# Another order of the expert passes in the first layer, two last passes summed on chip, and the latents' sum and norm ahead of the context's

## The chip, the cores and the metric

The kernel runs on one core of a Trainium2 chip. The metric is device time in microseconds (us) of one execution. Engines are named as in the profile: PE (TensorE; PEld is its weight load), DVE (VectorE), ACT (ScalarE), POOL (GpSimd) and SP (SyncE, which only issues DMAs here).

## The reference, cut to what matters

Two layers over 256 latent and 256 context tokens of width D = 1024 in float32. Each layer has a modulation (`w_mod`), an input projection in three groups of heads, attention, an output projection, and then a mixture of 32 experts (SwiGLU, hidden width 256) of which each token takes two. The output is the latent tokens alone, so the second layer's experts work on 256 tokens and the first layer's on 512. In short:

```python
for l in range(DEPTH):
    x, ctx = attention_block(x, ctx, c, c_ctx, l)    # w_mod, w_in, attention, w_out, DeepNorm
    for t in (x, ctx):
        gates, experts = route(t)                    # top group, then top-2 of its 8 experts
        y = sum(gates[k] * down(silu(up_a(t)) * up_b(t)) for k in experts)
        t = layernorm(ALPHA * t + g2 * y) * lg + lb  # g2 from w_mod, lg and lb from ln_rows
    ...
return x
```

## The kernel before, in words

**Memory.** All large tiles live in 23 units of 128 x 2048 floats (1 MB each), handed out by `Mem`. Weights are loaded in one fixed order (`stream`): `pump()` issues the next load as long as a unit is free and the weights held stay under a cap (`cap[0]`), and it is called after each `drop` of a weight that has been used. Weights of experts whose number is known at build time, and all weights of projections, are issued by SP (L161). The others of layer 0, 28 experts with three units each, are issued by POOL as indirect DMAs (L142), since the order of the experts by load is only known on the chip. An expert's units are called `c0` and `c1` (the two halves of up) and `c2` (down).

**Passes.** A pass is 128 rows of PE. `PLAN` gives their order: P is two experts with 64 rows each, Q four experts with 32 rows, F one expert with 128 rows, and f a second pass of 128 rows of the F before it, with the same weights, which are kept until f is done. Ahead of the list stand two P of fixed experts (the 2 in `PLAN`), so layer 0 has 14 passes, here P P Q F Q f P Q F Q P P P P. They are taken in sets of two, which share one one-hot matrix (`onehot`) and one gather of their rows by PE (`gather`, L1179).

**One pass.** `up` (L1192, with silu and product on ACT and DVE, L1198 and L1199), `mid` (two transposes, L1226), then in layer 0, for all passes but the last, `put`: down (L1237), and the 128 rows of results go to a DRAM buffer `ys` (L1242, by SP). The last pass stays on chip: `back` (L1210 to L1218), `down` (L1250, results split in a high and a low part, L1258 and L1259) and `combine` (L1273, L1278), which brings rows back to tokens by matmuls with the transposed one-hot.

**End of layer 0.** In the last pass, behind its `up`, `fold` reads the two rows of each token back from `ys` (8 indirect DMAs on POOL, L1465, two for each block of 128 tokens), and sums and scales them on ACT and DVE (L1469 to L1472) into the residual `X`. After `combine` comes `rest`, a loop for experts with more rows than their passes hold (L1478, L1479). Its number of turns is read on the chip and is 0 here, but entering it is a barrier for all engines, and what is behind it in the program stands behind it on every engine. Then layer 1 begins: `second` gives the DeepNorm of a block (L425 sum, L416 and L419 moments, L429 and L431, L436 the next norm), first for the two latent blocks. `presplit` splits the first projection weights (`qa`, L449 and L450), L320 multiplies `w_mod`, `turned` transposes the latents (L481 to L499), and L455 to L457 are the matmuls of the first projection. They are three float32r matmuls for one of float32.

**Order on an engine.** Each engine runs its instructions in the order in which a scheduler put them at build time; a scheduler's priority can be raised for a stretch of code (`high_priority`). A DMA is issued by its engine in that order too, and waits there for the memory it writes.

## Time and profile before

| | us |
|---|---|
| three runs | 1121.86, 1124.82, 1124.9 (median 1124.82) |
| profiled execution, own time | 1121.56 |
| its span, first to last instruction | 1119.8 |
| PE busy | 1000.2 (89%) |
| DVE, ACT, POOL busy | 510.2 (46%), 347.3 (31%), 303.3 (27%) |
| moved by DMA | 301.06 MB, mean 269 GB/s |

Busy times are shares of the whole span, over stages that have different limits. The experts of layer 0 run from about 330 to 638 us, layer 1 behind them, its experts to 1106 us. Line numbers (L142) are those of the kernel before, unless a sentence says that they are of the changed kernel.

### The profile page before, as it was taken

What the parts mean: (1) busy time and instruction counts of PE and PEld (TensorE: products, weight loads), DVE (VectorE), ACT (ScalarE), POOL (GpSimd) and SP (SyncE); (2) the same over time, 40 slices, a digit from 0 to 9 for tenths busy, and PEclk for the clock granted to TensorE, in tenths of its full rate; (3) what the DMA queues carried; (4) which work ended last, traced back from release to release, by engine and by line L of the source; (5) the groups of instructions that cost most, each with busy time, mean ns of one, the idle gap of its engine ahead of it and who ended that gap; (6) DMA issues with size and microseconds to landing.
All of it is one profiled execution on the core that took longest, in us unless ns stands there. A gap on an engine that the chain in (4) does not pass through costs nothing. (4 is left out here: it accounts for less than half of the span.)

```text
span 1119.8 us, 14771 instructions
## 1 busy us (share of the span) xinstructions
PE 1000.2 (89%) x5497; PEld 567.9 (51%) x5497; DVE 510.2 (46%) x1369; ACT 347.3 (31%) x707; POOL 303.3 (27%) x326
## 2 busy tenths in 40 slices
PE   4999999999999998999867279999998899999893
PEld 2788744557765553453212158854456554433231
DVE  5644367775575210100001887356665654342244
ACT  4533155553442110111000376134454221211011
POOL 2112134340002412434421222133210045443420
PEclk9999999999999999999999579999998799999997
DMA  9722157420469987899998563356425799999992
GB/s 381 304 73 91 43 207 285 176 76 1 170 272 364 421 357 299 354 422 423 421 421 351 215 221 119 112 201 241 165 76 225 286 363 419 421 421 421 421 421 95
DMA packets 46351, 301.06 MB, mean 269 GB/s; under 512 B 5410, under 2 KB 5794, under 8 KB 14532
## 3 DMA queue, kind: packets, MB, share of 16 engines
q0 software_dynamic: 25824, 177.81, 38.9%
q1 hardware_dynamic: 20452, 122.27, 28.8%
q8 instruction: 45, 0.74, 0.3%
q14 instruction: 30, 0.25, 0.1%
HBM read 292.19 MB, written 7.87 MB: 268 GB/s over the span
## 5 line engine op out<-in xcount | busy, mean ns | idle before, releaser
L142 POOL DMA_INDIRECT u<-in_w_exp,u x162 | 162.0, 1000 | 327.1 <-PE psa L1192 144.0
L1192 PE MATMUL psa<-u,u 128*32 128x512 f32 (+2 forms) x1040 | 221.3, 603 | 16.3 <-DMA u<-in_w_exp,u 16.2
L455 PE MATMUL psa<-u,u 128*128 128x512 f32 (+3 forms) x400 | 141.3, 356 | 1.0 <-ACT u L498 0.7
L456 PE MATMUL psa<-u,u 128*128 128x512 f32 (+3 forms) x400 | 140.4, 352 | 2.0 <-DVE u L450 2.0
L1192 PEld LDWEIGHTS psa<-u,u 128*32 128x32 f32 (+2 forms) x1040 | 65.5, 127 | 146.9 <-issue 109.9
L457 PE MATMUL psa<-u,u 128*128 128x512 f32 (+3 forms) x400 | 139.5, 352 | 0.4 <-DVE u L499 0.3
L1199 DVE TENSOR_TENSOR scr<-scr,psa 128x256 f32<-128x256 f32 x26 | 10.9, 420 | 213.1 <-ACT scr L1198 213.1
L1179 PEld LDWEIGHTS psc<-u,u 128*128 128x128 f32 x640 | 82.7, 197 | 31.5 <-issue 26.5
L878 POOL TENSOR_SCALAR u<-u,ri 128x512 f32<-128x512 f32 (+1 forms) x48 | 68.5, 1431 | 100.2 <-DVE ri L876 82.6
L1179 PE MATMUL psc<-u,u 128*128 128x256 f32 x640 | 92.7, 296 | 3.0 <-DVE u L1165 2.1
L455 PEld LDWEIGHTS psa<-u,u 128*128 128x128 f32 x400 | 75.7, 190 | 12.5 <-ACT u L498 1.1
L456 PEld LDWEIGHTS psa<-u,u 128*128 128x128 f32 x400 | 76.1, 190 | 11.7 <-DVE u L450 3.1
L457 PEld LDWEIGHTS psa<-u,u 128*128 128x128 f32 x400 | 75.6, 190 | 10.0 <-DVE u L499 0.9
L875 ACT ACTIVATE u<-psa,nm 128x512 f32<-128x512 f32 (+1 forms) x96 | 58.4, 615 | 55.8 <-DVE nm L873 50.9
L1198 ACT ACTIVATE scr<-psa 128x256 f32<-128x256 f32 x26 | 10.0, 385 | 192.1 <-PE psa L1192 192.1
L450 DVE TENSOR_TENSOR u<-u,u 128x1024 fp32r<-128x1024 f32 (+4 forms) x38 | 56.2, 1485 | 19.7 <-ACT u L449 19.6
L1237 PE MATMUL pse<-u,scr 128*32 128x512 f32 (+2 forms) x248 | 63.0, 600 | 1.9 <-ACT scr L1227 1.9
L1181 ACT ACTIVATE u<-psc 128x512 f32<-128x512 f32 x52 | 31.1, 597 | 107.9 <-PE psc L1179 69.4
L1250 PE MATMUL pse<-u,scr 128*64 128x512 f32 (+1 forms) x272 | 63.6, 599 | 0.6 <-DMA u<-in_w_exp,u 0.6
L873 DVE TENSOR_REDUCE nm<-psa 128x1 f32<-128x512 f32 (+1 forms) x80 | 53.1, 682 | 14.1 <-PE psa L863 10.5
L419 POOL TENSOR_TENSOR lns<-lns,mhalf 128x1 f32<-128x1 f32 x22 | 14.2, 646 | 149.0 <-DVE lns L418 108.3
L1273 PE MATMUL psa<-u,u 128*128 128x512 f32 x112 | 38.4, 458 | 17.1 <-DVE u L1278 11.0
(315 smaller groups left out, 1360.3 us busy)
## 6 DMA issues: line engine op xcount, KB each, us to landing
u<-in_w_mod SPq DMA_DIRECT2D x48, 1024.0 KB, 5.9
u<-in_w_exp SPq DMA_DIRECT2D x30, 1024.0 KB, 8.0
u<-in_w_out SPq DMA_DIRECT2D x8, 1024.0 KB, 5.0
ys<-u SPq DMA_DIRECT2D x13, 512.0 KB, 8.3
u<-in_w_in_b SPq DMA_DIRECT2D x10, 512.0 KB, 12.4
u<-in_w_in_v SPq DMA_DIRECT2D x4, 960.0 KB, 4.5
u<-in_w_in_qa SPq DMA_DIRECT2D x4, 768.0 KB, 10.4
u<-in_ln_rows SPq DMA_DIRECT2D x6, 512.0 KB, 5.8
```

Source lines behind the costliest of these rows:

```text
L142: G.indirect_dma_start(out=b.ap(UNIT), out_offset=None, in_=wexp_rows, in_offset=bass.IndirectOffsetOnAxis(ap=idx, axis=0), bounds_check=N ...
L450: V.tensor_tensor(l_[:, c], w[:, c], h[:, c].bitcast(F32), OP.subtract)
L455: PE.matmul(p, lhsT=a[0], rhs=b[0], start=first, stop=False)
L456: PE.matmul(p, lhsT=a[0], rhs=b[1], start=False, stop=False)
L457: PE.matmul(p, lhsT=a[1], rhs=b[0], start=False, stop=final)
L873: V.tensor_reduce(out=nm[:, s, 0:n], in_=pv, axis=AX.X, op=OP.max, negate=True)
L875: S.activation(P[:, i, :], pv[:, i, :], AF.Exp, bias=nm[:, s, i:i + 1], accum_out=su[:, s, i:i + 1])
L878: (G if s == 0 else V).tensor_scalar(P[:, i, :], P[:, i, :], ri[:, s, i:i + 1], None, op0=OP.mult)
L1179: PE.matmul(pv[:, j, :], lhsT=H[b][:, k * 128:(k + 1) * 128], rhs=OH[:, b, :], start=(b == 0 and i == 0), stop=(b == nb - 1 and i == 1))
L1192: PE.matmul(g[r, :], lhsT=XG[:, k, at * 128 + r.start:at * 128 + r.stop], rhs=W(t, k // 4).v(4, 512)[:, k % 4, :], start=(k == 0), stop=(k ...
L1237: PE.matmul(y[r, :], lhsT=hc[:, c * 128 + r.start:c * 128 + r.stop], rhs=W(t, 2).v(2, D)[:, c, f * 512:f * 512 + 512], start=(c == 0), sto ...
L1250: PE.matmul(y[r, :], lhsT=hc[:, c * 128 + r.start:c * 128 + r.stop], rhs=W(t, 2).v(2, D)[:, c, f * 512:f * 512 + 512], start=(c == 0), sto ...
```

## The change

The order of the passes in layer 0 becomes P P Q Q F f Q Q F P P P P P. Two passes stay on chip in place of one (`HOME`); each has its own split result (`parts`), and one PSUM sum takes both, four matmuls in place of two for a block and half. Twelve passes write to `ys`. The reads from `ys` (`fetch`) are issued at the start of the pass before the last and the fold stands behind that pass's up. The caps on the weights are 8 from the fourth last pass on (9 before), 7 from the one before the last (9), 4 in the last and 5 behind it (both as before). The loop `rest` stands ahead of the combine, with a result tile of its own. The combine is done for the two latent blocks first, then their DeepNorm with raised priority, then the combine for the two context blocks (`rest_of`). In passes with `put`, one piece of the next gather is ahead of `mid`.

```diff
-PLAN = ((2, "QFQfPQFQPPPP"), (3, "QPQPQPQPP"))
+PLAN = ((2, "QQFfQQFPPPPP"), (3, "QPQPQPQPP"))
...
-RP = (1, 1)
-LC = (4, 12)
+HOME = 2
+HC = (8, 7, 4, 5)
...
+        def make_h():
+            hT.extend([mem.get(UNIT, F32R) for _ in range(2)] for _ in range(2))
+            HT.extend([h.v(4, 512) for h in x] for x in hT)
+
+        if not last:
+            make_h()
...
-            together(*[before(b, xn) for b in range(2)])
+            with tc.high_priority(4000):
+                together(*[before(b, xn) for b in range(2)])
+            rest_of()
             for c in range(2):
                 presplit("qa", c)
+            make_h()
...
-        away = 0 if last else len(todo) - 1
+        away = 0 if last else len(todo) - HOME
...
+        def combine(pars, blocks=range(nb), final=False):
+
+            for b in blocks:
                 for f in range(2):
                     fs = slice(f * 512, f * 512 + 512)
                     p = bank("a")
...
+                    pairs = [(oht[j].v(nb, 128)[:, b, :], Y[:, f, :]) for j in pars for Y in parts(j)]
+                    for i, (o, y) in enumerate(pairs):
+                        PE.matmul(p, lhsT=o, rhs=y, start=(i == 0), stop=(i == len(pairs) - 1))
...
                     elif final:
+                        V.tensor_tensor(ACC[b][:, fs], p, BC["g2", b // 2][:, fs], OP.mult)
...
+        def rows_g2():
+            for t in range(2):
+                bc["g2", t] = mem.get(D)
+                BC["g2", t] = bc["g2", t].v(D)
                 mod_bcast(l, 5, t, BC["g2", t])
...
+        two = []
+
+        def fetch():
+
             for b in range(nb):
                 acc[b] = mem.get(D)
                 ACC[b] = acc[b].v(D)
+                two.append(mem.get(D))
                 for dst, j in ((ACC[b], 0), (two[b].v(D), 1)):
                     G.indirect_dma_start(out=dst, out_offset=None, in_=ys[:, :],
                                          in_offset=bass.IndirectOffsetOnAxis(ap=find[:, b, j:j + 1], axis=0),
                                          bounds_check=at_row, oob_is_err=False)
+
+        def fold():
...
+        def rest(dyn, par):
+
+            oht.append(mem.get(nb * 128, F32R))
+            parts(2)
             r = nc.values_load(lpi[0:1, 0:1], min_val=0, max_val=32)
...
+        end = len(todo) - 1
...
+            if i == end - 3:
+                cap[0] = HC[0] if not last else cap[0] - 2
+            if i == end - 1:
+                for k in [xg.pop((qe + 1) % 2), ohs.pop((qe + 1) % 2)] + yo:
+                    k.free()
+                if last:
+                    rows()
+                else:
+                    cap[0] = HC[1]
+                    rows_g2()
+            if i == end:
+                cap[0] = HC[2] if not last else 12
             if at_ == 0 and q < qe:
                 onehot(q + 1, [x[0:2] for x in sets[q + 1]])
+            if i == away and away:
+                fetch()
             hb = up(q, at_, n, m, W, rel)
...
+            if i == away and away:
                 fold()
+                rows()
...
+            pieces = [jj for jj in range(4 * at_, 4 * at_ + 4, 2) if q < qe]
+            if i < away and pieces:
+                gather(q + 1, len(sets[q + 1]), pieces.pop(0))
+            hc = mid(hb)
+            for jj in pieces:
+                gather(q + 1, len(sets[q + 1]), jj)
...
+                down(hc, ws, m, W, rel, i % 2)
+        held = [("exp", l, e + t, 2) for t in range(128 // m)]
+        rest(slot[held[0]], qe % 2)
+        for k in held:
+            drop(k)
+        pump()
+        fin = [end % 2] if last else [0, 1]
+        combine(fin, range(2), True)
+        for k in [iw] + xg + ohs + hh + [oht.pop(2), split_y.pop(2)]:
             k.free()
-        cap[0] = 5
+        cap[0] = HC[3]
...
+        def rest_of():
+
+            if not last:
+                combine(fin, range(2, nb), True)
+            for k in list(split_y.values()) + oht:
+                k.free()
```

POOL issues the weights of layer 0 and the reads from `ys` in one row. Before, all weights (`u_4542` to `u_4652` are the six of the last pass: `c0`, `c0`, `c1`, `c1`, `c2`, `c2`) stand ahead of the reads:

```order
L142 DMA u_4542<-in_w_exp,u_99 128x2048
L142 DMA u_4602<-in_w_exp,u_99 128x2048
L142 DMA u_4606<-in_w_exp,u_99 128x2048
L142 DMA u_4636<-in_w_exp,u_99 128x2048
L142 DMA u_4640<-in_w_exp,u_99 128x2048
L142 DMA u_4652<-in_w_exp,u_99 128x2048
L1465 DMA u_4706<-ys,find 128x1024
L1465 DMA u_3034<-ys,find 128x1024
L1465 DMA u_4713<-ys,find 128x1024
L1465 DMA u_4705<-ys,find 128x1024
```

In the changed kernel (L1480 is `fetch`, L1499 the loop) the eight reads stand between the last pass's two `c0` units and its `c1` and `c2` units, with the loop's entry behind:

```order
L142 DMA u_4528<-in_w_exp,u_99 128x2048
L142 DMA u_4588<-in_w_exp,u_99 128x2048
L142 DMA u_4592<-in_w_exp,u_99 128x2048
L1480 DMA u_4610<-ys,find 128x1024 x2
L1480 DMA u_4617<-ys,find 128x1024 x2
L1480 DMA u_4624<-ys,find 128x1024 x2
L1480 DMA u_4631<-ys,find 128x1024 x2
L142 DMA u_4647<-in_w_exp,u_99 128x2048
L142 DMA u_4659<-in_w_exp,u_99 128x2048
L142 DMA u_4663<-in_w_exp,u_99 128x2048
L142 DMA u_4726<-in_w_exp,u_99 128x2048
L1498 TENSOR_LOAD lpi
```

On POOL the last four weight units have thus moved behind the reads.

On DVE, in the changed kernel, between the split of the second last pass (L1269, into `u_4711`) and the silu product of the last pass (L1209), the whole fold stands (L1488 to L1490, four blocks):

```order
L1269 SCALAR_TENSOR_TENSOR u_4711<-pse,ws,u_4711 128x512
L589 TENSOR_TENSOR u_4730<-tab,tabl 128x64 x6
L1488 SCALAR_TENSOR_TENSOR u_4610<-u_4610,sc__2337 128x1024
L1489 TENSOR_TENSOR u_4610<-u_4610,u_4597 128x1024
L1490 SCALAR_TENSOR_TENSOR u_71<-u_71,u_4610 128x1024
...
L1490 SCALAR_TENSOR_TENSOR u_72<-u_72,u_4624 128x1024
L1489 TENSOR_TENSOR u_4631<-u_4631,u_4597 128x1024
L1490 SCALAR_TENSOR_TENSOR u_72<-u_72,u_4631 128x1024
L1209 TENSOR_TENSOR scr<-scr,psa 128x256
L1222 TENSOR_SCALAR u_3036<-psa,iop_87 128x512
L1228 TENSOR_REDUCE ws<-psa 64x1 x2
L1269 SCALAR_TENSOR_TENSOR u_4778<-pse,ws,u_4778 128x512 x2
```

The fold stood behind that product before; now the product, and all that follows it on DVE, is behind the fold.

On PE, at the edge between the layers, the row of before has the combine (L1273), the loop (L1479), and then the four units of `w_mod` (L320) with the transposes of the latents (L481) between them:

```order
L1273 MATMUL psa<-u_4772,u_3036 128x512 x16
L1478 TENSOR_LOAD lpi
L1479 COMPARE_AND_BRANCH
L1479 UNCONDITIONAL_BRANCH x2
...
L320 MATMUL pse<-u_5110,csil 32x512 x4
L320 MATMUL pse<-u_5112,csil 32x512 x4
L481 MATMUL psc<-ident,u_4706 128x128 x2
L320 MATMUL pse<-u_5130,csil 32x512 x4
L481 MATMUL psc<-ident,u_4713 128x128
...
L481 MATMUL psc<-ident,u_4713 128x128
L455 MATMUL psa<-u_5102,u_5049 128x384
```

In the changed kernel the loop (L1499) comes first, then the combine of all four blocks (L1282), the four units of `w_mod` together, and only then the transposes (L487) and the first projection (L455):

```order
L1498 TENSOR_LOAD lpi
L1499 COMPARE_AND_BRANCH
L1499 UNCONDITIONAL_BRANCH x2
...
L1282 MATMUL psa<-u_4711,u_3036 128x512 x2
L1282 MATMUL psa<-u_4778,u_3036 128x512 x2
...
L1282 MATMUL psa<-u_4711,u_3036 128x512 x2
L1282 MATMUL psa<-u_4778,u_3036 128x512 x2
L320 MATMUL pse<-u_5132,csil 32x512 x4
L320 MATMUL pse<-u_5134,csil 32x512 x4
L320 MATMUL pse<-u_5144,csil 32x512 x4
L320 MATMUL pse<-u_5158,csil 32x512 x4
L487 MATMUL psc<-ident,u_4610 128x128 x2
...
L455 MATMUL psa<-u_5124,u_5146 128x384
```

The combine has moved behind the loop, and the transposes behind all four units of `w_mod`.

SP's row has moved too: before, two `ln_rows`, a `cq`, two `qa`, a `cq` and a `b` are issued among the last writes of `ys`; in the changed kernel all of them but the first `qa` wait for memory that is free only when the last pass's up is done.

## Rows read from the trace of the kernel before

**Rows 1.** The page, part 1: busy time, share of the span, instructions.

```profile
PE 1000.2 (89%) x5497; PEld 567.9 (51%) x5497; DVE 510.2 (46%) x1369; ACT 347.3 (31%) x707; POOL 303.3 (27%) x326
```

**Rows 2.** Stretches of core 0: length, busy us (x count), granted clock, DMA share, GB/s.

```profile
540.00:560.00 20.00, 15.89 (x68) 5.21 (x66) 1.31 (x3) 1.37 (x3) 8.91 (x9) 1.00 1.01 421
...
600.00:620.00 20.00, 13.29 (x50) 5.18 (x50) 4.09 (x8) 3.18 (x5) 6.82 (x7) 0.83 0.80 293
620.00:640.00 20.00, 5.74 (x10) 2.66 (x10) 17.88 (x20) 5.41 (x7) 2.82 (x4) 0.50 0.47 173
640.00:660.00 20.00, 10.44 (x51) 3.68 (x52) 17.84 (x43) 11.61 (x18) 5.98 (x8) 0.56 0.79 284
...
700.00:800.00 100.00, 98.22 (x485) 57.11 (x484) 54.68 (x136) 33.42 (x83) 26.29 (x26) 1.00 0.52 183
```

**Rows 3.** Timeline of PE: start, us, line, out<-in, count, idle before and its releaser.

```profile
601.75 5.34 PE L1192 MATMUL psa<-u,u 128*64 128x512 f32 x14 [3.23 <-DMA u<-in_w_exp,u]
...
609.33 3.70 PE L1250 MATMUL pse<-u,scr 128*64 128x512 f32 x16
...
634.72 2.07 PE L1273 MATMUL psa<-u,u 128*128 128x512 f32 x4 [0.51 <-DVE u L1278]
643.59 1.94 PE L320 MATMUL pse<-u,csil 128*32 128x512 f32 x8 [6.79 <-DVE lns L415]
...
659.41 0.42 PE L455 MATMUL psa<-u,u 128*128 128x384 f32 x1
```

**Rows 4.** Waits of PE, 330 to 612: us in total, times, longest.

```profile
PE psa L1192 <- DMA u<-in_w_exp,u: 15.0, 9, 3.2
```

**Rows 5.** Timeline of the DMA issues of SP, 566 to 662.

```profile
593.28 0.70 SPq L161 DMA_DIRECT2D u<-in_w_in_cq  x1
...
638.31 10.61 SPq L161 DMA_DIRECT2D u<-in_w_mod  x4
```

**Rows 6.** DMA engines, 395 to 470, in 40 slices: busy tenths, GB/s.

```profile
DMA  9999999999460000389999999999119999999999
GB/s 419 419 419 424 395 409 424 428 419 419 197 267 0 0 0 0 57 293 367 371 402 428 428 433 411 424 433 384 52 22 197 315 411 424 424 417 430 437 424 433
```

**Rows 7.** Timeline of POOL, 395 to 470.

```profile
424.81 0.99 POOL L142 DMA_INDIRECT u<-in_w_exp,u  x1 [20.40 <-PE psa L1192]
...
449.53 0.99 POOL L142 DMA_INDIRECT u<-in_w_exp,u  x1 [11.04 <-PE pse L1237]
```

**Rows 8.** Timeline of POOL, 566 to 662.

```profile
611.36 0.99 POOL L1465 DMA_INDIRECT u<-ys,find  x1 [23.67 <-DMA u<-in_w_in_kc]
...
620.50 1.49 POOL L1465 DMA_INDIRECT u<-ys,find  x1 [0.30 <-DMA u<-ys,find]
```

**Rows 9.** Timeline of DVE, 600 to 662.

```profile
618.05 1.28 DVE L1470 SCALAR_TENSOR_TENSOR u<-u,sc__2337,u 128x1024 f32<-128x1024 f32 x1 [4.36 <-DMA u<-ys,find]
...
632.85 1.21 DVE L1472 SCALAR_TENSOR_TENSOR u<-u,u 128x1024 f32<-128x1024 f32 x1
633.98 3.67 DVE L1278 TENSOR_TENSOR u<-psa,u 128x512 f32<-128x512 f32 x6
639.74 1.22 DVE L425 SCALAR_TENSOR_TENSOR u<-u,u 128x1024 f32<-128x1024 f32 x1 [2.08 <-issue]
```

**Rows 10.** Timeline of ACT, 600 to 662.

```profile
654.68 1.24 ACT L436 ACTIVATE u<-u,lns 128x1024 f32<-128x1024 f32 x1 [1.76 <-DVE lns L435]
```

**Rows 11.** DMA issues, 560 to 612: count, KB each, median us to landing.

```profile
u<-in_w_in_qa SPq DMA_DIRECT2D x2, 768.0 KB, 9.1
u<-in_ln_rows SPq DMA_DIRECT2D x2, 512.0 KB, 9.7
u<-in_w_in_cq SPq DMA_DIRECT2D x2, 512.0 KB, 12.0
ys<-u SPq DMA_DIRECT2D x2, 512.0 KB, 12.7
```

**Rows 12.** The page, part 6: DMA issues: count, KB each, median us to landing.

```profile
ys<-u SPq DMA_DIRECT2D x13, 512.0 KB, 8.3
```

More of the change, by code (lines that the diff above doesn't have):

```diff
@@ L457, in three, with layer @@
         PE.matmul(p, lhsT=a[1], rhs=b[0], start=False, stop=final)
-    def layer(l, first, before=None, after=None):
+    def layer(l, first, before=None, after=None, rest_of=None):
         nb = 4 if l == 0 else 2
@@ L1262, in layer @@
         total = t3("total", 2, 2)
-        def combine(par, first=False, final=0):
-            OT = oht[par].v(nb, 128)
-            YHI, YLO = parts()
-            for b in range(nb):
+        def combine(pars, blocks=range(nb), final=False):
+            for b in blocks:
                 for f in range(2):
@@ L1448, in rows @@
         def rows():
-            for k in ([] if last else [("g2", 0), ("g2", 1)]) + ["lg", "lb"]:
+            for k in ("lg", "lb"):
                 bc[k] = mem.get(D)
@@ L1454, in rows @@
                 (G if last else SP).dma_start(out=BC[k], in_=ins["ln_rows"][l, 2 + j:3 + j, :].to_broadcast([128, D]))
-            for t in range(0 if last else 2):
+        def rows_g2():
+            for t in range(2):
+                bc["g2", t] = mem.get(D)
+                BC["g2", t] = bc["g2", t].v(D)
                 mod_bcast(l, 5, t, BC["g2", t])
-        def fold():
-            two = [mem.get(D) for _ in range(nb)]
+        two = []
+        def fetch():
             for b in range(nb):
@@ L1490, in rest @@
                 hb = up(par, 0, 1, 128, lambda t, c: dyn, lambda c: load(c + 1))
[L1491 to L1495 removed]
+                ws = back(par, 0, 1, 128, 35, 2)
+                down(mid(hb), ws, 128, lambda t, c: dyn, lambda c: None, 2)
+                combine([2])
+        end = len(todo) - 1
         for i, (m, col, e, _, go) in enumerate(todo):
@@ L1503, in rel @@
             def rel(c):
-                if go and (i != at_rest or c < 2):
+                if go and (i != end or c < 2):
                     for t in range(128 // m):
@@ L1507, in rel @@
                     pump()
-            def others():
-                held = [("exp", l, e + t, 2) for t in range(128 // m)]
-                rest(slot[held[0]], i % 2 if i < len(todo) - 1 else 0, 2 if i == len(todo) - 1 else 0)
-                for k in held:
-                    drop(k)
-                pump()
-            if i == len(todo) - 4:
-                cap[0] -= 2
-            if i == len(todo) - 1:
-                cap[0] = LC[l]
-            if i == len(todo) - 2:
-                xg.pop((qe + 1) % 2).free()
-                ohs.pop((qe + 1) % 2).free()
-                rows()
+            if i == end - 3:
+                cap[0] = HC[0] if not last else cap[0] - 2
@@ L1526, in layer @@
             hb = up(q, at_, n, m, W, rel)
-            if i and i - 1 != at_rest and i > away:
-                combine((i - 1) % 2, i == 1)
-            if i == len(todo) - 1 and not last:
-                for k in yo:
-                    k.free()
+            if i and not away:
+                combine([(i - 1) % 2])
+            if i == away and away:
                 fold()
+                rows()
             if i == 1:
                 lists()
-            hc = None if i < away else mid(hb)
@@ L1536, in layer @@
-            if q < qe:
-                for jj in range(4 * at_, 4 * at_ + 4, 2):
-                    gather(q + 1, len(sets[q + 1]), jj)
+            pieces = [jj for jj in range(4 * at_, 4 * at_ + 4, 2) if q < qe]
[4 more added lines that the diff above has]
+                gather(q + 1, len(sets[q + 1]), jj)
             if i < away:
-                put(i, mid(hb), m, W, rel)
+                put(i, hc, m, W, rel)
@@ L1541, in layer @@
             else:
                 ws = back(q, at_, n, m, col, i % 2)
-                down(hc, ws, m, W, rel)
-            if i == at_rest and i < len(todo) - 1:
-                combine(i % 2)
-                others()
-        combine((len(todo) - 1) % 2, False, 1)
-        if at_rest == len(todo) - 1:
-            others()
-        for k in split_y + [iw] + xg + ohs + oht + hh:
+                down(hc, ws, m, W, rel, i % 2)
+        held = [("exp", l, e + t, 2) for t in range(128 // m)]
+        rest(slot[held[0]], qe % 2)
@@ L1563, in done @@
                 k.free()
-        return second, done
+        return second, done, rest_of
     for g in (1, 2):
@@ L1571, in backbone @@
         fillers.append(lambda j=j: (one(j), two(j)))
-    before, after = layer(0, mod0_steps(0, "e"))
+    steps = layer(0, mod0_steps(0, "e"))
     for g in (1, 2):
         fillers.extend(mod_steps(1, g))
-    before, after = layer(1, None, before, after)
+    before, _, _ = layer(1, None, *steps)
     together(*[before(b, {}) for b in range(2)])
```

48 lines of the change are left out of this document (20 added, 28 removed).

## The prediction

> **What bounds the kernel now.** I read the page first [rows 1]: TensorE (PE) is busy 89% of the span, so what can be won is in the 120 us in which it isn't. The table by stretches [rows 2] says where those are: the last four passes of the first layer's experts (540 to 607, PE busy three quarters, DMA share 1.0) and the edge between the two layers (607 to 659, PE busy 5.74 of 20 us and 10.44 of 20). From 700 on PE is busy 98% of the time with the DMA half idle. So the reader is to see two limits, one behind the other.
>
> Up to the end of the last up-projection (call it T; 601.75 + 5.34 = 607.1 [rows 3]) the limit is the stream of expert weights. In 330 to 612 PE waited nine times for a weight unit, 15.0 us in all, 3.2 at most [rows 4]; it had just waited 3.23 for the last one [rows 3]. In that stretch the DMA engines moved 421 GB/s with no gap [rows 2], which is 2.49 us for a unit of 1.049 MB, 1.25 for 0.524 MB and 1.87 for 0.786 MB; these three are the prices of the stream below. A unit that meets an empty queue takes longer: `w_mod` issued at 638.31 [rows 5] was multiplied at 643.59 [rows 3], 5.3 us.
>
> The stream itself had one hole, far ahead of its end. In the view of the DMA engines over 395 to 470 (1.875 us a slice) the rate falls from 420 to nothing between 414 and 434 and once more, to 22, between 446 and 455 [rows 6]. What each slice lacks of 420, summed from the one of 197 to the one of 371 and then from 384 to 315, is 9.0 slices or 17 us. POOL shows why: it had waited 20.40 us for PE to free memory before its issue at 424.81, and 11.04 before that at 449.53 [rows 7]. Those are the passes F and f: F gives nothing back since f uses its weights again, and only one Q (12 units given back) stands ahead of each.
>
> From T to the first projection of layer 1 (L455 at 659.41 [rows 3]) is 52.3 us, a chain over all engines: down (609.33, 3.70), reads of `ys` issued only from 611.36 [rows 8], the fold on DVE from 618.05 to 634.06 [rows 9] with the combine matmuls waiting in it, the last L1278 to 637.65, the loop's barrier to 639.74 [rows 9], the sums and norms of the latents to 655.92 (L436, [rows 10]), transposes, L455.
>
> **The change, part by part.** First T, which moves as the landing of the last `c1` unit (601.7) moves.
>
> 1. *Order QQFfQQFPPPPP.* Two Qs put 24 returned units ahead of F and f, in place of 12. Following the list by hand (a unit is issued when its memory is given back, lands 2.49 after the one before it, but not under 5.3 after its issue), the holes shrink to one of some 3.5 and one of 0.9 us at the end of f: 4.4 in place of 17, so -12.6. Bounds: -17 (no hole is left) and -6 (the two Q pairs, which take 60 us of stream for 31 us of PE, leave POOL as late again as before). I take -12.6.
> 2. *One ys write less* (12 for 13): -1.25.
> 3. *Prefetch moved behind T.* Before, two `ln_rows`, one `cq` and two `qa` landed ahead of that unit, 1.049 + 0.524 + 1.573 = 3.15 MB or 7.5 us of the stream; the second `cq` (issued 593.28, 12.0 to landing) and `b` came after it [rows 5, 11]. Now SP's queue has only the first `qa` (1.87) ahead of T: -5.6.
> 4. *Reads of ys ahead of the last four units* on POOL: 8 of 0.524 MB: +10.0. They need pass 11's write landed (8.3 us in the median, 12.7 for the last two, [rows 11, 12]). Between the last two weights of that pass and the last `c1` lie ten units, the reads, a write and a `qa`: 24.9 + 10 + 1.25 + 1.87 = 38 us of stream, so the write goes out about T - 35, has landed by T - 27 to T - 22, and eight issues of 1.29 (0.99 and 0.30 between, [rows 8]) end at T - 17 to T - 12. The two `c1` units issued next have to land by T - 5.3, so be issued by T - 10.6: they just are. For the issues' slower pace and a late start I add 1.4 (from 0 to 6).
> 5. *Caps 8 and 7 for 9*: a unit is issued later, but with 3 to 12 us still queued at each issue this costs nothing. Uncovered, each group of releases would cost 5.3 - 2.49 = 2.8.
> 6. *The fold moved under pass 13's up.* Its 12 DVE instructions of 1.21 to 1.28 [rows 9] are 15 us, and stand in DVE's queue ahead of the product behind pass 13's up. The first reads land some 6 us after issue, so the fold runs from about T - 16 to T - 1: hidden, just. A read later by x delays T's successors by about x.
>
> Sum for the last `c1`: 601.7 - 12.6 - 1.25 - 5.6 + 10.0 + 1.4 = 593.7; the up behind it took 5.34 at a granted clock of 0.83 [rows 2, 3], so T = 598.4 to 599, 8.6 us earlier. Bounds with those of 1 and 4: 592.5 to 610.
>
> DVE also has POOL's four last issues beside the fold. In the row at 620.50 such an issue, run beside fold instructions, took 1.49 in place of 0.99 [rows 8]: 4 x 0.5 = 2.0 us at most by that. The Trainium skill (SBUF — State Buffer, "Who interferes with whom") has it that a DVE instruction with two SBUF inputs and a GpSimd one that reads SBUF exclude each other for a whole instruction; by that it would be up to 4 x 1.28 = 5.1 us. The trace shows the smaller one, so I keep it inside the 1.4 of step 4, and the larger in a rival.
>
> **From T on**, in place of 52.3:
>
> 7. *Down and split*: 609.33 + 3.70 is T + 5.9, plus the split on DVE and ACT, some 1.5: T + 7.5, as before but with no fold between.
> 8. *Loop first.* Its barrier took 2.09 from the last DVE instruction (637.65 to 639.74, [rows 9]): T + 9.6 by that. But it waits for every outstanding load too, and the seven now behind T on SP (`qa`, two `ln_rows`, two `cq`, two `b`: 0.786 + 6 x 0.524 = 3.93 MB) are 9.3 us plus 2 of start: T + 11.3. I take T + 11.5; the loads cost 2.
> 9. *Combine of the latents*: a group of four L1273-like matmuls took 2.07 at half clock [rows 3]; four groups 8.3, then the last product 0.6, L425 1.22: T + 21.6.
> 10. *Norms*: from the end of the second L425 (639.74 + 2 x 1.22 = 642.2) to the end of the second L436 (655.92) it was 13.7 us with both blocks in step [rows 9, 10]; block 0 is now 4.1 ahead, so 10 to 12: T + 32.5.
> 11. *PE's own queue*: behind all eight groups (8 x 2.07, T + 28.1) stand four units of `w_mod`. Three are loaded behind the barrier, the fourth waits for the first one's matmuls (1.94, [rows 3]) and lands 5.3 later: T + 35.3; its own matmuls (1.2 to 1.9) and the transposes behind them, which stood between them before, with scaling and splitting some 3.5: first L455 at T + 40.5. PE's queue, not the norm chain, ends last. The `w_mod` wait is what is late next.
>
> So 52.3 becomes 40.5: -11.8. The bounds are T + 34 (chain of step 10 alone) and T + 48 (both waits in a row, barrier later by 4).
>
> *Behind the edge* nothing new: PE is busy 98% from 700 on [rows 2], so an earlier start is carried through; `kc` and `b` load some 15 us nearer to their use, and I price that at 0 to +2. At the end the loop also stands ahead of the combine, which exchanges two steps of one chain: 0.
>
> **Sum**: -8.6 - 11.8 = -20.4 on the profiled execution's own 1121.6: 1101.2. The median of three is 1124.8, 3.3 above it, the fastest like it; I put the forecast between, at 1103, and the rivals' times on the same scale, 1.8 above their sums.
>
> **Rivals.**
>
> (a) *The reads and the fold hold T.* The write lands in 12.7, the reads begin at T - 22, POOL's last four issues each wait out a DVE instruction (4 x 1.28), the fold ends after T. T gives back 4 to 8 of the 8.6: about 1109. For it: the 12.7 and the 1.49; against: one issue beside the fold cost 0.5, not 1.28.
>
> (b) *More than that*: with no hole left (-17) T is 594 to 595, with the barrier held by DVE alone and the fourth `w_mod` not last, T + 36: 13 + 16 = 29, about 1094.
>
> (c) *The order does nothing*: the stream is late again at the second pair of Qs; step 1 is worth 0. T = 601.7 - 1.25 - 5.6 + 10.0 + 1.4 + 5.34 = 611.6, the edge still 40.5: 7.3 us gained, 1116.
>
> (d) *Slower.* With the caps 8 and 7 the queue runs empty at each release in passes 10 to 13, so that a unit lands 5.3 after its issue and not 2.49 after the one before it. It decides from 8 such groups on (8 x 2.8 = 22); all of the nine, with the reads of step 4 then exposed as well (+10), are 35: 1121.6 - 20.4 + 35 is 1136, on the scale 1138. Against it: the 421 GB/s of [rows 2], which stays unless 3 to 12 us of queue are gone.
>
> **How the numbers follow.** The likeliest 0.55, for 1103 (own range 1097 to 1108); (a) 0.2; (b) 0.12; (c) 0.07; (d) 0.04; and 0.02 for nothing measurable. The range holds the first three but for the far end of (b): 1093 to 1114. Of (c) 0.02 end within 0.3% (3.4 us, about what a measurement of this kernel can tell from no change) and 0.01 beyond: faster 0.91, within 0.3% 0.04, slower 0.05.
>
> **What would show it.** Step 1: no slice of the DMA view between 400 and 470 falls to nothing for over 4 us, and the weights of pass 9 land 12 us earlier. Steps 3, 4: `fetch` (L1480 of the changed kernel) is issued before 585 and its reads are landed before T; SP issues the second `qa` just at T. Step 6: the fold's last row (L1490 there) ends before the silu product of pass 13. Steps 7 to 11: barrier 11.5 after T, L320's fourth unit as the last wait ahead of the transposes, L455 at T + 40.5. The forecast is wrong if T isn't at 594 to 604, or if the combine's groups don't run back to back behind the barrier.

## The result, and the profile after

The changed kernel took 1103.11, 1104.6, 1104.96 and 1108.46 us, median 1104.78, against 1124.84 before: ratio 0.9833, 95% interval 0.9803 to 0.9862. Run again beside the experiments it had 1102.23 (ratio 0.9795, 0.9766 to 0.9824). So it is faster by some 20 us, as forecast (1103). The way there was another one than forecast: T, the end of the last up-projection of layer 0, hardly moved, and the edge behind it gave all of it.

The profiled execution is the longest of the four (1108.46, span 1106.6). Everything in it, and in the second profile, stands 3.8 us later than before from the first up on. Kernels whose program is the same up to there have that first up anywhere from 342.9 to 346.2, so the change need not be the cause, though both profiles of the changed kernel have it; below, T is therefore also given from the first up.

The stretches of the changed kernel, with the columns of [rows 2]:

```profile
540.00:560.00 20.00, 18.50 (x84) 6.91 (x83) 1.72 (x3) 1.36 (x3) 9.91 (x10) 1.00 1.01 421
...
580.00:600.00 20.00, 5.35 (x21) 1.44 (x17) 13.65 (x19) 5.97 (x6) 10.53 (x9) 0.75 1.02 413
600.00:620.00 20.00, 13.21 (x47) 4.35 (x48) 6.61 (x10) 2.14 (x4) 0.00 (x0) 0.73 0.63 246
620.00:640.00 20.00, 14.92 (x69) 8.65 (x70) 17.29 (x49) 11.21 (x17) 6.45 (x9) 0.78 0.85 335
640.00:660.00 20.00, 18.64 (x114) 16.82 (x112) 17.89 (x41) 16.48 (x26) 6.23 (x5) 0.88 0.46 165
700.00:800.00 100.00, 98.16 (x491) 52.59 (x490) 56.63 (x139) 38.25 (x93) 29.15 (x25) 1.00 0.50 170
```

PE now has its empty stretch ahead of T (5.35 of 20 us between 580 and 600) and is busy 14.92 and 18.64 of 20 between 620 and 660, where it was 5.74 and 10.44 [rows 2]. The timeline of PE, as in [rows 3]:

```profile
582.35 3.65 PE L1202 MATMUL psa<-u,u 128*64 128x512 f32 x14 [0.65 <-DMA u<-in_w_exp,u]
601.87 1.97 PE L1202 MATMUL psa<-u,u 128*64 128x512 f32 x2 [15.87 <-DMA u<-in_w_exp,u]
605.63 6.13 PE L1202 MATMUL psa<-u,u 128*64 128x512 f32 x14 [1.80 <-DMA u<-in_w_exp,u]
...
613.94 3.70 PE L1260 MATMUL pse<-u,scr 128*64 128x512 f32 x16
619.83 9.17 PE L1282 MATMUL psa<-u,u 128*128 128x512 f32 x32 [2.19 <-DVEq L1499]
628.93 2.78 PE L320 MATMUL pse<-u,csil 128*32 128x512 f32 x24
634.97 1.93 PE L320 MATMUL pse<-u,csil 128*32 128x512 f32 x8 [3.25 <-DMA u<-in_w_mod]
637.75 0.69 PE L487 MATMUL psc<-ident,u 128*128 128x128 f32 x2 [0.85 <-ACT u L436]
...
643.18 0.67 PE L455 MATMUL psa<-u,u 128*128 128x384 f32 x1
```

The last up waited 15.87 us for its `c1` units and ended at 605.63 + 6.13 = 611.76 (607.1 before). From there to the first L455 it is 31.4 us where it was 52.3. What stood ahead of those units shows in the issues of SP and POOL, as in [rows 5] and [rows 8]:

```profile
581.04 4.48 SPq L161 DMA_DIRECT2D u<-in_w_in_qa  x2
586.30 0.33 SPq L1463 DMA_DIRECT2D u<-in_ln_rows  x1
590.94 0.33 SPq L161 DMA_DIRECT2D u<-in_w_in_cq  x1
596.44 0.33 SPq L1463 DMA_DIRECT2D u<-in_ln_rows  x1
600.24 0.33 SPq L161 DMA_DIRECT2D u<-in_w_in_cq  x1
611.79 0.80 SPq L161 DMA_DIRECT2D u<-in_w_in_b  x2
```

```profile
576.23 0.99 POOL L1480 DMA_INDIRECT u<-ys,find  x1 [13.27 <-DVE scr L1209]
...
585.30 1.85 POOL L1480 DMA_INDIRECT u<-ys,find  x1 [0.30 <-issue]
587.45 0.99 POOL L142 DMA_INDIRECT u<-in_w_exp,u  x1 [0.30 <-issue]
...
590.04 1.75 POOL L142 DMA_INDIRECT u<-in_w_exp,u  x1 [0.30 <-issue]
```

Two `qa`, two `ln_rows` and two `cq` were issued from 581 to 600, and the eight reads from 576 to 585, all ahead of T; only `b` waited for T. What let the two `ln_rows` and the two `cq` go shows in the timeline of DVE, in the first of the three fold instructions of each block:

```profile
584.99 1.28 DVE L1488 SCALAR_TENSOR_TENSOR u<-u,sc__2337 128x1024 f32<-128x1024 f32 x1 [1.62 <-DMA u<-ys,find]
...
589.63 1.28 DVE L1488 SCALAR_TENSOR_TENSOR u<-u,sc__2337 128x1024 f32<-128x1024 f32 x1 [0.84 <-DMA u<-ys,find]
...
595.13 1.28 DVE L1488 SCALAR_TENSOR_TENSOR u<-u,sc__2337 128x1024 f32<-128x1024 f32 x1 [1.70 <-DMA u<-ys,find]
...
598.93 1.28 DVE L1488 SCALAR_TENSOR_TENSOR u<-u,sc__2337 128x1024 f32<-128x1024 f32 x1 [1.25 <-DMA u<-ys,find]
```

Each of the four was issued 0.03 us behind the end of one of these (586.27, 590.91, 596.41, 600.21), which is the last to read one of the two tiles that the reads fill for a block.

The DMA engines over 395 to 470, as in [rows 6], have lost most of their hole: what the slices lack of 420 is 3.3 slices or 6.2 us, where it was 17.

```profile
DMA  9999999999999999999999999999999985299999
GB/s 424 415 424 419 419 389 258 306 402 428 433 419 437 419 419 424 424 419 424 424 419 419 424 409 435 441 424 419 424 380 343 352 332 218 74 267 350 402 424 428
```

The fold's last instruction and the product behind the last up on DVE, as in [rows 9], show the fold hidden:

```profile
602.52 1.23 DVE L1490 SCALAR_TENSOR_TENSOR u<-u,u 128x1024 f32<-128x1024 f32 x1
612.22 0.42 DVE L1209 TENSOR_TENSOR scr<-scr,psa 128x256 f32<-128x256 f32 x1 [8.47 <-ACT scr L1208]
...
625.08 1.22 DVE L425 SCALAR_TENSOR_TENSOR u<-u,u 128x1024 f32<-128x1024 f32 x1
...
639.75 1.22 DVE L425 SCALAR_TENSOR_TENSOR u<-u,u 128x1024 f32<-128x1024 f32 x1
```

### The profile page after: what moved, and what is told of

The parts are those of the page before. It is cut to its first block, busy times and chain, and to the rows that moved or that the text cites. A ratio compares the mean times of both kernels' runs of the same rounds, so it can differ in the third digit from the quotient of the medians.

```text
span 1106.6 us, 14809 instructions
## 1 busy us (share of the span) xinstructions
PE 998.9 (90%) x5525; PEld 577.0 (52%) x5525; DVE 512.7 (46%) x1364; ACT 349.3 (32%) x708; POOL 305.2 (28%) x325
## 5 line engine op out<-in xcount | busy, mean ns | idle before, releaser
L1202 PE MATMUL psa<-u,u 128*32 128x512 f32 (+2 forms) x1040 | 218.1, 602 | 23.8 <-DMA u<-in_w_exp,u 23.7
L1202 PEld LDWEIGHTS psa<-u,u 128*32 128x32 f32 (+2 forms) x1040 | 65.5, 127 | 152.7 <-issue 110.6
L455 PE MATMUL psa<-u,u 128*128 128x512 f32 (+3 forms) x400 | 142.8, 360 | 0.9 <-ACT u L504 0.7
L1209 DVE TENSOR_TENSOR scr<-scr,psa 128x256 f32<-128x256 f32 x26 | 10.9, 421 | 168.5 <-ACT scr L1208 168.5
L456 PEld LDWEIGHTS psa<-u,u 128*128 128x128 f32 x400 | 77.3, 193 | 12.9 <-DVE u L450 4.2
L455 PEld LDWEIGHTS psa<-u,u 128*128 128x128 f32 x400 | 77.1, 193 | 11.5 <-ACT u L504 1.1
L457 PEld LDWEIGHTS psa<-u,u 128*128 128x128 f32 x400 | 76.5, 192 | 9.8 <-issue 1.2
L1260 PE MATMUL pse<-u,scr 128*64 128x512 f32 (+1 forms) x288 | 67.4, 599 | 0.6 <-DMA u<-in_w_exp,u 0.6
L1191 ACT ACTIVATE u<-psc 128x512 f32<-128x512 f32 x52 | 31.1, 597 | 101.9 <-PE psc L1189 59.6
L1247 PE MATMUL pse<-u,scr 128*32 128x512 f32 (+2 forms) x232 | 57.3, 600 | 1.4 <-ACT scr L1237 1.4
L449 ACT ACTIVATE u<-u 128x1024 fp32r<-128x1024 f32 (+4 forms) x38 | 47.5, 1266 | 14.2 <-PE psa L456 4.6
## 6 DMA issues: line engine op xcount, KB each, us to landing
u<-in_w_in_b SPq DMA_DIRECT2D x10, 512.0 KB, 11.8
```

The source lines that it names most:

```text
L455: PE.matmul(p, lhsT=a[0], rhs=b[0], start=first, stop=False)
L456: PE.matmul(p, lhsT=a[0], rhs=b[1], start=False, stop=False)
L457: PE.matmul(p, lhsT=a[1], rhs=b[0], start=False, stop=final)
L1202: PE.matmul(g[r, :], lhsT=XG[:, k, at * 128 + r.start:at * 128 + r.stop], rhs=W(t, k // 4).v(4, 512)[:, k % 4, :], start=(k == 0), stop=(k ...
L1247: PE.matmul(y[r, :], lhsT=hc[:, c * 128 + r.start:c * 128 + r.stop], rhs=W(t, 2).v(2, D)[:, c, f * 512:f * 512 + 512], start=(c == 0), sto ...
L1260: PE.matmul(y[r, :], lhsT=hc[:, c * 128 + r.start:c * 128 + r.stop], rhs=W(t, 2).v(2, D)[:, c, f * 512:f * 512 + 512], start=(c == 0), sto ...
```

## The experiments

What follows reads off each profile: the start of the first up of layer 0, T, the time from the one to the other, the first combine behind T, the first L455, and the edge from T to it (us). Medians and ratios to the kernel before come from the runs beside it in the same session (before: 1123.85, 1124.29 and 1126.61 in three sessions).

| kernel | first up | T | T - first up | combine | L455 | edge | median | ratio (95%) |
|---|---|---|---|---|---|---|---|---|
| before | 342.05 | 607.09 | 265.0 | 612.96 | 659.41 | 52.3 | 1124.84 | 1 |
| changed | 345.82 | 611.76 | 265.9 | 619.83 | 643.18 | 31.4 | 1104.78 | 0.9833 (0.9803-0.9862) |
| after_again | 345.99 | 609.35 | 263.4 | 617.48 | 640.43 | 31.1 | 1102.23 | 0.9795 (0.9766-0.9824) |
| after_old_order | 343.14 | 616.78 | 273.6 | 624.92 | 648.26 | 31.5 | 1111.46 | 0.9891 (0.9858-0.9924) |
| before_new_order | 342.95 | 593.05 | 250.1 | 598.92 | 646.34 | 53.3 | 1112.13 | 0.9894 (0.9866-0.9922) |
| weights_first | 342.86 | 588.25 | 245.4 | 612.28 | 637.55 | 49.3 | 1101.27 | 0.98 (0.9769-0.983) |
| prefetch_held | 345.34 | 599.61 | 254.3 | 613.06 | 638.67 | 39.1 | 1099.91 | 0.9773 (0.9739-0.9806) |
| loop_last | 344.55 | 607.38 | 262.8 | 609.50 | 646.68 | 39.3 | 1107.59 | 0.9839 (0.9805-0.9873) |
| blocks_together | 344.99 | 604.98 | 260.0 | 613.39 | 640.95 | 36.0 | 1102.96 | 0.9812 (0.9778-0.9846) |
| short_fold | 343.67 | 589.39 | 245.7 | 609.09 | 636.19 | 46.8 | 1103.58 | 0.9813 (0.9781-0.9846) |
| caps_lower | 346.20 | 610.87 | 264.7 | 619.89 | 642.69 | 31.8 | 1105.67 | 0.981 (0.9781-0.9839) |
| all_behind | 344.79 | 589.25 | 244.5 | 602.26 | 630.79 | 41.5 | 1093.2 | 0.9703 (0.9681-0.9725) |
| all_behind_mod | 345.35 | 587.46 | 242.1 | 600.47 | 628.44 | 41.0 | 1096.47 | 0.9736 (0.9717-0.9755) |

The changed kernel once more, unedited (after_again).

> The changed kernel once more, nothing edited, for a second profile. In its first profile everything stood 3.7 us later than in the profile of before from the first 30 us on, ahead of any changed work. Both theories: the median stays at 1103 to 1106. If the late start is only the run's own, a faster profile has T (end of the last up of layer 0) at 608 and the first L455 at about 639.5; if it belongs to the changed program, every profile has its first up at 345 to 346 and not 342.

The late first up came again (345.99), so whether it belongs to the run or to the program stays open. T is 263.4 behind it, some 2.5 us less than in the first profile, and the median is just under what was expected. loop_last and blocks_together below are edited behind T alone, and have T 262.8 and 260.0 behind the first up. So the same work up to T took from 260.0 to 265.9 us in four profiles, 263.0 in the mean, and what a single profile says of T is uncertain by some 3 us. Differences at T are taken from that mean below.

The order of the passes, undone in the changed kernel and done alone in the kernel before:

```diff
-PLAN = ((2, "QQFfQQFPPPPP"), (3, "QPQPQPQPP"))   # after_old_order: changed kernel
+PLAN = ((2, "QFQfPQFQPPPP"), (3, "QPQPQPQPP"))
...
-PLAN = ((2, "QFQfPQFQPPPP"), (3, "QPQPQPQPP"))   # before_new_order: kernel before
+PLAN = ((2, "QQFfQQFPPPPP"), (3, "QPQPQPQPP"))
...
-                cap[0] -= 2
+                cap[0] -= 3
```

> The changed kernel with the old order of passes alone (QFQfPQFQPPPP). Theory 1 (the weight stream bounds T; the new order took 11 us of empty DMA time out of it, and the reads ahead of the last four units put 10 back): T 10 to 12 us later than in the changed kernel, with the edge from T to the first L455 unchanged at some 31 us, so 1115 us. Theory 2 (the stream is late anyhow behind the second pair of Qs, the order does nothing): 1103 to 1107, T unchanged.

> The kernel before with the new order of passes alone (its cap from the fourth last pass on is 8 and not 9, since the layer-1 tiles do not fit otherwise). Theory 1: T 10 to 12 us earlier, the edge of 52 us unchanged, 1113 us. Theory 2: 1122 to 1125. If both parts of the change are worth their own and add up, this gain and that of the changed kernel with the old order make 20 us.

Theory 1 held in both as to T and the edge. Undone, T is 10.6 us later (8 to 14 against the four profiles) and the edge the same 31.5, though the median lies between the two forecasts; done alone, T is 15 us earlier (265.0 to 250.1, one profile each) and the edge 53.3 for 52.3. In the old order the DMA engines of the changed kernel show the holes of [rows 6] again:

```profile
GB/s 424 419 419 419 419 393 422 439 428 424 332 70 253 0 0 0 0 35 245 406 363 393 433 428 428 402 428 424 419 74 4 175 336 413 422 426 422 428 428 428
```

In time the order is worth 9.2 us in the changed kernel and 11.7 in the kernel before. So it was carried through; what took back at T in the changed kernel what the order had given, the next two experiments show. The parts don't quite add up: 11.7 and the 12.4 of the change under the old order make 24.1, where both together gave 21.6.

The reads behind the last weights (weights_first):

```diff
-            if i == away and away:
+            if i == end and away:
                 fetch()
...
-            if i == away and away:
-                fold()
-                rows()
...
                 down(hc, ws, m, W, rel, i % 2)
+            if i == end and away:
+                fold()
+                rows()
```

> The changed kernel with the eight reads of ys behind the last pass's weights (issued at the start of the last pass) and the fold behind its down. Theory 1 (4 MB of reads ahead of the last units hold T): T 8 to 10 us earlier, at some 598 to 600, but the fold and with it the loop's barrier end later than T + 8, at T + 14 to 18, so that 0 to 3 us are left: 1102 to 1106. Rival (T is held by something else, the prefetch on SP or the caps): T less than 3 us earlier, and the kernel 5 to 10 us slower, for the fold stands in the open again.

T went 17.6 us earlier (15 to 21), twice what was expected, and the whole of it was given back by the edge: PE waited 16.84 us for the barrier, and that for the fold, whose last instruction ended at 611.64. The last `cq` ahead of the barrier, issued at 608.14, landed at 611.5, so the loads would have held it nearly as long.

```profile
584.61 3.65 PE L1202 MATMUL psa<-u,u 128*64 128x512 f32 x14 [1.31 <-DMA u<-in_w_exp,u]
...
612.28 10.09 PE L1282 MATMUL psa<-u,u 128*128 128x512 f32 x32 [16.84 <-DVEq L1499]
```

```profile
596.66 1.28 DVE L1488 SCALAR_TENSOR_TENSOR u<-u,sc__2337 128x1024 f32<-128x1024 f32 x1 [1.43 <-DMA u<-ys,find]
...
610.42 1.22 DVE L1490 SCALAR_TENSOR_TENSOR u<-u,u 128x1024 f32<-128x1024 f32 x1
```

The median is that of the changed kernel within its interval. T is thus held by what stands ahead of the last weights, but T alone is worth nothing when the fold comes last at the barrier.

The prefetch held back to T (prefetch_held), all else as changed:

```diff
+            if late[0] and key[0] != "exp":          # in pump(); late from pass end - 1 on
+                return
...
+                if gate[0] is not None:              # also for lg and lb in rows()
+                    V.tensor_copy(b.ap(n)[:, 0:1], gate[0])
                 SP.dma_start(out=b.ap(n), in_=ap)
...
-                rows()                               # behind fold()
...
+            if i == end and not last:                # behind up()
+                late[0], gate[0] = False, hb[:, 0:1]
+                rows()
+                pump()
             hc = mid(hb)
```

> The changed kernel, in which no layer-1 tile (qa, ln_rows, cq, b) is loaded ahead of the silu product of the last pass: one column of that product is copied into each tile ahead of its load. In the changed kernel qa, qa, ln_rows, cq, ln_rows (3.15 MB, 7.5 us of the stream) were issued by SP between 581 and 600, ahead of the last c1 unit, where the prediction had them behind T. Theory 1 (each MB ahead of the last units moves T by 2.4 us): T 5 to 7.5 us earlier against the first up (257 to 260 us behind it, 263 to 266 in the changed kernel); the edge grows by 3 to 6, since qa, ln_rows and cq now come behind T and w_mod behind those, so 1099 to 1103 in all. Theory 2 (the reads alone, or POOL's issues, hold T): T moves by under 2 us and the kernel is 3 to 6 us slower, 1106 to 1109.

T is 8.8 us earlier (6 to 12) and the wait for `c1` 9.04 us for 15.87; theory 2 is out. Theory 1 had counted five tiles; the six that were issued ahead of T are 3.67 MB, which at its rate of 2.4 us for 1 MB is 8.8. The tiles now stand ahead of the barrier instead: SP issues them from 600.74, and the combine begins at 613.06, 13.4 us behind T, with nothing running on DVE for the 5.87 us until 612.88. SP's wait at the loop, between 602 and 612.5, ended with the landing of a `qa`, at 611.7 (us in total, times, longest):

```profile
SPq L1506 <- DMA u<-in_w_in_qa: 8.5, 1, 8.5
```

The issues of SP and the row of PE:

```profile
600.74 0.89 SPq L1470 DMA_DIRECT2D u<-in_ln_rows  x2
601.74 0.92 SPq L166 DMA_DIRECT2D u<-in_w_in_qa  x2
612.47 0.81 SPq L166 DMA_DIRECT2D u<-in_w_in_cq  x2
```

```profile
591.63 1.97 PE L1207 MATMUL psa<-u,u 128*64 128x512 f32 x2 [9.04 <-DMA u<-in_w_exp,u]
594.13 5.48 PE L1207 MATMUL psa<-u,u 128*64 128x512 f32 x14 [0.53 <-DMA u<-in_w_exp,u]
...
613.06 10.03 PE L1287 MATMUL psa<-u,u 128*128 128x512 f32 x32 [7.56 <-issue]
```

Of some 9 us at T about 2 to 5 are left in time. The loop's place and the blocks' order at the edge:

```diff
-        rest(slot[held[0]], qe % 2)                  # loop_last
+        fin = [end % 2] if last else [0, 1]
+        combine(fin, range(nb if not last else 2), True)
+        rest(slot[held[0]], qe % 2)
...
-        combine(fin, range(2), True)                 # blocks_together
+        combine(fin, range(nb), True)
...
-            with tc.high_priority(4000):
-                together(*[before(b, xn) for b in range(2)])
+            together(*[before(b, xn) for b in range(2)])
```

> The changed kernel with the loop behind the combine of all four blocks, as it was before (then the norms). By the trace the combine then ends at T + 17.5 and the barrier at T + 19.5, where the first L425 stood at T + 13.3 to 15.7: 4 to 6 us slower than the changed kernel, 1107 to 1109. Rival (the loop's place is worth nothing, since the barrier only changes places with the combine and the wait for w_mod ends last): w_mod is loaded 9 us later, so this rival would need L455 at T + 31 all the same: within 1 us of the changed kernel.

> The changed kernel with all four blocks combined ahead of the norms and no raised priority (the loop stays first). PE's order is the same; on DVE four more products of 0.68 us stand ahead of or between the latents' norms. If the latents' chain ends last at the edge: 2 to 3 us slower, 1105 to 1107. If the fourth w_mod unit ends last: no change, 1102 to 1105.

With the loop last the edge is 8 us longer (39.3) and the kernel 5 slower than after_again; the rival is out, for `w_mod` came later with it (issued 624.03, its first matmul at 629.86). But this edit also takes all four blocks ahead of the norms, as blocks_together does, so not all of it is the loop's place: against blocks_together it is 3.3 us of edge and 4.6 of the median. With the blocks together and the loop first the edge grew by 4.6, yet the median (1102.96) is that of the changed kernel: T was 3 to 6 us earlier in that profile, for no reason that its edit gives, so what the latents' turn is worth in time stays open between 0 and 4.6.

Caps one lower (caps_lower, `HC = (7, 6, 4, 5)`):

> The changed kernel with the caps one unit lower (7 and 6 for 8 and 7): a weight unit is issued one release later. Step 5 of the prediction (3 to 12 us are still queued at each issue, so the caps cost nothing): T within 2 us of the changed kernel (260 to 266 us behind the first up), 1101 to 1105. Rival (d) (the queue runs empty at each group of releases): each of nine groups costs up to 2.8 us more, T 8 us or more later, 1110 or more.

T is where it was (264.7) and the median, 1105.67, 0.7 above the range: the caps hold nothing up at T, and the mechanism of rival (d) isn't there at this size.

What these runs point to is to have only weights and reads in the stream ahead of the barrier, and little on DVE. First the fold with one DVE instruction for three (short_fold, on weights_first):

```diff
                 V.scalar_tensor_tensor(ACC[b], two[b].v(D), sc_[:, b, 3:4], ACC[b], op0=OP.mult, op1=OP.add)
-                V.tensor_tensor(ACC[b], ACC[b], BC["g2", b // 2], OP.mult)
-                V.scalar_tensor_tensor(X[b], X[b], ALPHA, ACC[b], op0=OP.mult, op1=OP.add)
...
-                        V.tensor_tensor(ACC[b][:, fs], p, BC["g2", b // 2][:, fs], OP.mult)
+                        V.tensor_tensor(ACC[b][:, fs], ACC[b][:, fs], p, OP.add)
+                        V.tensor_tensor(ACC[b][:, fs], ACC[b][:, fs], BC["g2", b // 2][:, fs], OP.mult)
```

> The kernel with the weights ahead of the reads, and in the fold only the first of its three DVE instructions for a block: the product with g2 is taken once, behind the combine (on the sum of both parts), and the residual's scale in the norm's first instruction. Ahead of the barrier DVE then has 3.8 us for 15. The barrier was 24 us behind T there and ended with the fold (611.6). Theory 1 (the fold on DVE holds the barrier): barrier 5 to 8 us earlier, 2.4 us given back for the products behind it: 1095 to 1098. Rival (the landing of the reads or of SP's tiles holds it): barrier under 3 us earlier, 1100 to 1103.

A miss: the barrier came 4.3 us sooner behind T (19.7 for 24.0), between the two forecasts, and 2.5 were left at the edge, but nothing in time. DVE ended its work ahead of the barrier at 604.1 and stood idle for 4.75 us. The loads held it: the last read of `ys`, issued at 593.17 with two `b` behind it (599 to 602), landed at 607.5, the second `b` at 607.8, and the fold of the read's block stands behind the barrier. SP's wait at the loop, between 602 and 608.6:

```profile
SPq L1498 <- DMA u<-ys,find: 5.3, 1, 5.3
```

So the last two kernels also keep every layer-1 tile behind the loop and take the reads' tiles in another order, all_behind_mod with `w_mod` ahead of `cq` in the stream:

```diff
+            late[0], gate[0] = False, X[0][:, 0:1]   # behind rest(); in pump() and rows() as in prefetch_held
+            rows()
         pump()
+        gate[0] = None
```

> Weights ahead of the reads, the short fold, and in addition no layer-1 tile (qa, ln_rows, cq, b) loaded ahead of the loop: one column of the residual, read behind the loop, is copied into each tile ahead of its load. Theory 1 (up to the barrier only the stream of weights and reads and the fold on them count; behind it there is room for 5 MB under the norms): T stays at 245 us behind the first up, the reads land some 6 us earlier than with weights_first (by 594), the barrier is at T + 13 to 16 in place of T + 24, and the first L455 stands 24 to 28 us behind the barrier: edge 38 to 43, 1091 to 1096 in all. Rival (the loads only change places: qa, cq, b and w_mod, 7.9 MB behind the barrier, end last at the edge): edge 46 to 50, 1100 to 1104.

> As all_behind, with the four w_mod units ahead of cq and b in the stream. Theory 1: w_mod then lands 5 us earlier and its matmuls stand ahead of the transposes again; if w_mod ends last in all_behind it is 2 to 4 us faster, else within 1.5 us of it. Rival as there.

all_behind is the fastest, 1093.2, 3% under the kernel before, and its interval lies clear of the changed kernel's. T is as early as in weights_first (244.5) and the combine begins 13.0 us behind it, as theory 1 had it; but the last read landed at 600.7 and not by 594, and it is what ACT, POOL and SP wait for at the loop:

```profile
585.60 3.65 PE L1207 MATMUL psa<-u,u 128*64 128x512 f32 x14 [1.31 <-DMA u<-in_w_exp,u]
...
602.26 8.28 PE L1287 MATMUL psa<-u,u 128*128 128x512 f32 x28 [7.13 <-issue]
...
622.67 0.69 PE L492 MATMUL psc<-ident,u 128*128 128x128 f32 x2 [9.04 <-ACT u L441]
...
630.79 0.42 PE L460 MATMUL psa<-u,u 128*128 128x384 f32 x1
```

PE's long wait there is now the 9.04 us for the norm of the latents (ACT). all_behind_mod has the same edge (41.0) and is 3 us slower, which neither theory had. Its profile loses more than that in layer 1, where from L455 to the end it is 462.3 us against 455.7; that stretch is from 453.0 to 462.3 in the profiles of all these kernels, and the cause is open.

## Why the prediction was right in time and wrong on the way

The sum was -8.6 at T and -11.8 at the edge, -20.4. Measured, T is +0.9 and -1.7 from the first up in the two profiles, the edge -20.9 and -21.2, and layer 1 gives back 3.0 and 1.5 (from L455 to the last instruction 455.1 us before, 458.1 and 456.6), which is within its spread. The total is right because two errors of 7 to 9 us cancel. Some 3 us of that hang together, as step 8 below shows; the rest is luck. By the prediction's own sign ("wrong if T isn't at 594 to 604") its way failed: T was at 611.8 and 609.4, or at 608.0 and 605.4 with the first up where it was before.

**Step 3 failed**: "Prefetch moved behind T ... SP's queue has only the first `qa` (1.87) ahead of T". The order shows `qa` to `cq` behind the release of the last pass's units, and I read this as behind T, in what stands ahead of the prediction too. But a load waits for its memory alone. The second `qa` waited for matmuls of the last up (L1202) and was issued at 585.19, while the first half of that up still ran (to 586.0). The two `ln_rows` and two `cq` took tiles of the reads, which L1488 gives back block by block: the fold that step 6 moved ahead of T let them go there. All six were issued by 600.24, 3.67 MB. prefetch_held shows their price at T, 8.8 us, where step 3 had 1.87. With 8.8 the prediction's T, 256.4 behind the first up, becomes 263.3, and 263.0 is the mean of the four profiles; with all six out it becomes 254.5, and prefetch_held has 254.3. So step 3 is the whole error at T, as far as single profiles can tell.

The other terms of T: the order (step 1, -12.6) gave 15.0 alone and 10.6 with the rest of the change, within its bounds. The reads (step 4, +10.0 + 1.4) were sized about right: the four kernels with the weights first have T 242.1 to 245.7 behind the first up, 18.6 us under the 263.0 in the mean, for reads and prefetch together; less the 8.8 that is 9.8. Counted from the first up the reads were also issued when step 4 had them (the first at 230.4, forecast 229 to 234); that they stand at T - 36 to T - 25 is because T came later. Caps (step 5) are as forecast, and the fold (step 6) is hidden, earlier than forecast (T - 27 to T - 8): it ended at 603.75, the product behind it came at 612.22. Step 2 wasn't tried.

Of POOL's five issues beside the fold two took longer, 1.85 and 1.75 for 0.99, 1.6 us in all. These two began while an L1488 ran (585.30 and 590.04, with 0.97 and 0.87 us of it left) and were longer by 0.86 and 0.76; the other three began with at most 0.08 us of a DVE instruction left. So an issue waited for what was left of the instruction that it met, less some 0.12 us. The 1.49 of [rows 8] is the same: that issue, at 620.50, met this instruction with 0.63 us left and was longer by 0.50, so what the prediction took for a price, 0.5 and not a whole 1.28, was the rest of an instruction.

```profile
619.91 1.22 DVE L1471 TENSOR_TENSOR u<-u,u 128x1024 f32<-128x1024 f32 x1
```

The Trainium skill (SBUF — State Buffer, "SBUF: two separate sides") has it that of a DVE instruction with two SBUF inputs and a GpSimd one that reads SBUF, whichever starts first holds the shared ports for the whole instruction and the other blocks. The issue is one that reads SBUF (its row numbers are in `find`). The trace agrees for POOL, with the numbers above; on DVE's side it shows no wait (L1490 at 587.57 took its 1.22 beside the issue of 587.45).

**The edge was overpriced in three steps.** Step 8: the barrier was at T + 8.1, not T + 11.5. That is the other side of step 3's error, since the tiles had landed ahead of it; in prefetch_held, where they do come behind T, it is at T + 13.4. Step 9: 32 matmuls of the combine took 9.17 us and not 16.6. I took 2.07 for four from a row in which PE stood between waits at half clock; run back to back behind the down they took 0.29 each, at a mean granted clock of 0.81. Step 11: with that, the fourth `w_mod` unit was multiplied at T + 23.2 (T + 35.3 forecast), and was not last: the transposes waited 0.85 and 0.98 us for L436 (step 10's chain, 11.2 us behind the second L425, as forecast). L455 came at T + 31.4, not T + 40.5.

Rival (a) named the place (what stands ahead of the last units gives T back) but not the cause: the reads cost what step 4 had for them, POOL's issues 1.6 us, and the fold ended 8 us ahead of T; the prefetch held T, which no rival had. Rival (c) is out by both order experiments; (d) by caps_lower. Of (b) the second half came true, the barrier held by DVE alone and the fourth `w_mod` not last, but not its T.

## What to carry to other kernels

Where the DMA stream is the bound, 1 MB ahead of the last unit that is waited for costs 2.4 us there (3.67 MB cost 8.8), whoever issues it; so write down for each load what frees its memory, not where its issue stands in the program. A gain at one point (18 us at T here) is worth only what the next common point, here the loop's barrier, lets through: look at what else arrives there, loads included. Take an instruction's duration from a row in which its engine is as busy as it will be.

## What the runs showed of the hardware

A loop of no turns is a barrier whose price depends on what is under way, loads included. From the end of DVE's last instruction ahead of it to PE's first one behind it, it took 0.68 us in the changed kernel (617.50 + 1.65 to 619.83) and 0.64 in weights_first, where DVE came last. It took 1.9 in all_behind, 4.95 in short_fold and 6.1 in prefetch_held (607.01 to 613.06). In these three ACT, POOL and SP waited for a load to land, at 600.7, 607.8 and 611.7, and PE began 1.3 to 1.6 us behind that.

An issue of an indirect DMA on POOL waits for the DVE instruction that it meets, if that reads two tiles in SBUF. Between 560 and 640 us, in eight of the profiles, 16 issues began while a fold instruction ran with 0.20 to 1.00 us left, and each took longer than 0.99 by what was left less 0.12 to 0.13 us. Three that began within 0.03 us of a fold instruction's start took 0.99. With one input in PSUM there is no such wait: over the whole of the 13 profiles 137 issues met a TENSOR_TENSOR of that kind (`u<-u,psa`) with over 0.15 us left, and all took 0.99.

PE came out of the 15.87 us wait slowly: two matmuls took 1.97 and the next 14 took 6.13, where the first half of the same up took 3.65 for 14. The granted clock was 1.00 in that first half (582.3 to 586.0) and 0.50, the lower of the levels of 1.2 and 2.4 GHz, from 591 to 610.6, with PE idle from 586.0 to 601.87. In weights_first, with a wait of 1.31 and the clock at 1.00, the second half took 3.65 as well. So of this long wait some 2.5 us came on top.

The first up of layer 0 stands at 342.1 to 346.2 us in the 13 profiles, and the runs of the kernel before lie from 1121.5 to 1129; a few us between two profiles mean nothing unless both are counted from the same event, and even then the same work up to T differed by up to 6 us.
